# Token-sum rows split at every second first gate product, up weights tied from the 21st product on, two steps of the cached pieces moved to the sample block

## The chip, the cores and the metric

The kernel runs on one core of a Trainium2 chip. The metric is the device time of one execution in microseconds (us); lower is better. The engines are TensorE (PE, with its weight loads PEld), VectorE (DVE), ScalarE (ACT), GpSimd (POOL) and SyncE (SP), whose queue issues nearly all DMAs. Each engine works through its own instructions in order and waits for the others by semaphores.

## The reference

One inference step of a decoder layer, for 1024 prompt tokens and 64 sample tokens (8 sequences of 8), in float32. Cut to what matters:

```python
u = rms_norm(x, ln1)
a, q, k, v, g_a, g_b = split(u @ w_in)             # 512, 768, 768, 768, 1024, 1024 columns
q, k = rms_norm(heads(q), q_norm), rms_norm(heads(k), k_norm)     # 12 heads of 64
A = ((trailing_means(a) - a) @ lin per group) * pool_scale @ w_pa
# three groups of 4 heads: (window, dilation) = (128, 1), (512, 4), (2048, 16)
B = combine(dilated_window_attention(q, k, v)) @ w_pb  # sample tokens also read cached keys and values
h = x + (sigmoid(g_a) * A + sigmoid(g_b) * B) @ w_o
y = h + square(relu(rms_norm(h, ln2) @ w_up)) @ w_down           # 4096 hidden columns
```

It also returns the new pooling states and the updated key and value windows of both groups of tokens.

## The kernel before, in words

All 1088 tokens lie side by side as columns (features on the partitions). A float32 product is made of three passes over two halves of each operand: a high part, rounded by ACT (`split` L114, `put` L1255), and a low part, the difference, made by DVE (L115, L1256). The passes are high-high, high-low of one side, and high-low of the other; in the products of the later stages (`products`, L1248) the weights' low half is read in the last third of each half of the tokens.

The stages in order: the pooling input (PE at L319, to 61 us), q, k and v of the head groups 2, 1 and 0 with the attention woven in (61 to 383 us), the gates (383 to 580), A and B (L1566, to 653), the output projection (`ph`, to 751), the up projection (`pz`, to about 1096) and the down projection (`pd`, L2020, to the end). Gates, up and down use a two-by-two block scheme with seven block products, whose operands include sums and differences of the two token halves and of blocks of weights.

**What sets the order.** PE's instructions stand in the order of the code. The other engines' instructions are put in order by the framework's scheduler, from their dependencies and a timeline that it simulates. `behind_pe(ins)` adds a dependency: `ins` may not start before the matmul that was issued last in the code (`last_mm`). That is the kernel's means of keeping early work from crowding out urgent work.

**Group 0's blocks and the cached pieces.** The loop over blocks (L1137 and on) goes through (8, 0), 1, 2, 3, 4, 5, 6, 7: block 8 is the sample tokens, the others are 128 prompt tokens each. For each block the products of q, k and v are made (`qkv_part`), narrow ones one by one, wide ones (q and k together) for blocks 1 to 5. Behind each product DVE makes `ms`, POOL `mr` = ms ** -0.5 (L634), and ACT rescales with it (L639). `sample_own_keys` (L828 and on) is a generator that works through the sample tokens' cached keys of group 2 in 16 pieces, then their values in 16 pieces, one piece per step: it issues the two loads of the next piece, has POOL multiply the present one in four instructions (L839 `pck`, L863 `pcv`), and at the next step DVE adds it up (L841, L866, L867). Between keys and values lies a softmax (L849 to L854). `own_step` takes one step; the condition `own` says after which products (group, block, part 0/1/2 for q/k/v) it is taken.

**The gates.** `order` lists 16 first gate products, n = 0 to 15, which need no sums; at each, weights of product n + 3 are made ready (`raw_gf`), and the results are copied out (`g`, L1474). Meanwhile the four feature blocks k = 0 to 3 of the token sums are loaded (`fetch_sums`, tiles `gv` with one buffer each, k = 3 computed from x itself at L1325 to L1330) and split into the planes that the later gate products read (`split_sums`: four high and four low halves and a subtraction for each k). `split_t4` splits the eighth sum (`gt`). Then `gate_group` makes the other products, whose weights are sums (`sm_g`, L1400) put into `gapart` and `places` tiles. The attention's last part is woven into the first products; there PE's transpose `twg0u` (L760) reads `hl` (high half ACT L734, low half DVE L735).

**The up projection.** A queue of products is worked off by `run`, which prepares the weights three products ahead. Products 0 to 11 are the first two of each of six groups; 12 to 16 are the rest of group 0. `make_versions` at the start of the stage normalizes the second token half and makes its sums and differences in wide steps of 1088 columns (L1652, L1735, L115). The weights go through five places in turn (`up_spots`); their high halves (in `put_up`) and the weight sums (L1836, `sm`) are tied by `in_time`:

```python
    def in_time(ins):
        if begun[0] > 2:
            behind_pe(ins)
```

`begun[0]` is the number of the product being prepared, so before the change all but the first three wait for the product that PE was given last.

Of the kernel before, what the change touches and what calls it, by code (L numbers as in the profile page):

```python
# [36 lines left out]
def decoder_step(ctx, tc, i, o):  # L37
# [91 lines left out]
    def gate_quarter(f, a):  # L129
        return gate_panel(f).rearrange("p (k n) -> p k n", k=KD)[:, 4 * a:4 * a + 4, :P]  # L130
# [8 lines left out]
    def line_up(src, name, *after, width=None):  # L139


        wt = places[:, place[0] % 3]
        place[0] += 1
        width = width or src.shape[1]
        for a, key in zip(range(0, width, 512), after):
            coming_up.append(dict(width=width, src=src, name=name, a=a, key=key, wt=wt, raw=None))
        ask_ahead()
        return wt
# [33 lines left out]
    def behind_pe(ins, mm=None):  # L182

        tc.add_manual_dep(ins.ins, (mm or last_mm[0]).ins.name,
                          mybir.DependencyInfo(mybir.DependencyClass.Sync, mybir.DependencyReason.DATA), reason="pace")
# [361 lines left out]
    def step():  # L547
        for f in [later.pop(0) for _ in range(len(later))]:
            f()
        for r in list(active):  # L550
            if next(r, True):
                active.remove(r)
        cool[0] -= 1
        for r in waiting[:2]:
            if r not in primed:
                primed.add(r)
                next(r)
        if waiting and cool[0] <= 0:
            r = waiting.pop(0)
            if not next(r, True):  # L560
                active.append(r)
            cool[0] = 2

    def qkv_tiles(name, sample):
        qk = rr(ap1, [P, 512], F32, name=f"qk{name}", tag="qk", bufs=2)
        if sample:
            return qk, rr(ap1, [P, 256], F32, name=f"v{name}", tag="vs", bufs=2)
        return qk, rr(ap, [P, 256], F32, name=f"v{name}", tag="v", bufs=4)
# [16 lines left out]
    def in_order(blk):  # L585

        for s, copy in ((1, s_.copy), (0, v_.tensor_copy)):
            for k in range(0, KD, 2):
                t = natt[:, 4 * s + k // 2]
                copy(t.rearrange("p k (l r) -> p k l r", r=4),  # L590
                     act_t[s].rearrange("p k (r l) -> p k l r", r=4)[:, k:k + 2, blk * 32:(blk + 1) * 32, :].bitcast(F32))
                nat[s, k], nat[s, k + 1] = t[:, 0, :], t[:, 1, :]
# [484 lines left out]
    def own_step(every):  # L1077
        count[0] += 1
        if count[0] % every == 0:
            if next(own_keys, True) is not None and (2, "own") not in done:  # L1080
                done.add((2, "own"))
# [25 lines left out]
    for g in (2, 1, 0):  # L1107
# [39 lines left out]
        for blks in ((8, 0), (1,), (2,), (3,), (4,), (5,)) + (((6, 7),) if g else ((6,), (7,))):  # L1147

            if g and 6 in blks:
                next_wts = [(place[0] + j) % 3 for j in range(3)]  # L1150
                for j, after in enumerate((((7, 0), (6, 1), (6, 1), (7, 1)), ((7, 1), (6, 2), (6, 2), (7, 2)), ((7, 2),) * 4)):
                    line_up(i["w_in"][2 + 3 * j + g - 1], f"qkv{g - 1}_{j}", *((g,) + a for a in after))
            elif 7 in blks:
                wg_first = line_up(lambda a: gate_quarter(a // 512 % 2, a // 1024), "ga0",
                                   *((0, 7, j) for j in (0, 0, 1, 1)), width=2048)
            tiles = {b: qkv_tiles(f"{g}_{b}", b == 8) for b in blks}

            for js in (((0, 1), (2,)) if blks[0] in (1, 2, 3, 4, 5) else ((0,), (1,), (2,))):
                for b in (blks[::-1] if g == 0 and js == (2,) else blks):

                    own = g < 2 and b < 8 and (g, b, js) not in ((1, 7, (1,)), (1, 6, (2,)), (1, 7, (2,)))

                    def middle():
                        step()
                        if own:
                            own_step(1)

                    if g == 1 and extra and (1, "keys") in done:
                        extra = []
                        natt = np_.tile([P, 8, 2, P], F32R, name="natt", tag="nat")  # L1170
                        in_order(0)
                    wide = len(js) == 2
                    qkv_part(g, wts, b, f"{g}_{b}", tiles[b], js, middle if wide else None)
                    feed()
                    if own and not wide:
                        own_step(1)
                    if g < 2 and b == 8 and 0 in js:
                        dma(wrow, src_w)
                    if g == 0 and b == 8 and 2 in js:

                        sel = ap0.tile([P, 1024], F32R, name="sel", tag="smp")[:, :12 * HD]
                        behind_pe(v_.tensor_tensor(
                            sel.rearrange("p (a d) -> p a d", d=HD),
                            ident[:, :12].unsqueeze(2).to_broadcast([P, 12, HD]),
                            ident[:, 12:24].unsqueeze(2).to_broadcast([P, 12, HD]), op=ALU.add))
                    if 2 in js:
                        (sample_block if b == 8 else prompt_block)(g, b, *tiles[b])
                if g == 2 and 2 in js and 8 in blks:
                    start(pool_branch(), "p", now=True)
                    start(token_sums(), "t", now=True)  # L1190
# [76 lines left out]
    got, begun = {}, [0]  # L1267

    def in_time(ins):

        if begun[0] > 2:
            behind_pe(ins)

    def run(ahead=3):
# [33 lines left out]
    def fetch_sums(k):  # L1308
        if k == 3:
            rows_of[k] = [gx.tile([P, TOK], F32, name=f"gx{a}") for a in range(2)]  # L1310
            for a, x in enumerate(rows_of[k]):
                dma(x, i["xT"][:, 4 * a + k, :])
            return
        rows_of[k] = [rr(gx, [P, H], F32, name=f"gv{n}_{k}", tag=f"gv{n}", bufs=1) for n in range(3)]
        for t, slot in zip(rows_of[k], (0, 3, 1)):
            dma(t, ts_d[k][:, slot])

    def split_sums(k):

        v = rows_of[k]  # L1320
        if k == 3:
            v = [rr(gx, [P, H], F32, name=f"gv{n}_{k}", tag=f"gv{n}", bufs=1) for n in (0, 1, 3, 2)]
            for a, x in enumerate(rows_of[k]):
                for j in range(2):
                    v_.scalar_tensor_tensor(two(v[2 * a + j]), by_token(x, j), ln1[:, 4 * a + k:4 * a + k + 1], two(rb_g[j]),  # L1325
                                            op0=ALU.mult, op1=ALU.mult)
            v_.tensor_tensor(v[0], v[1], v[0], op=ALU.subtract)
            v_.tensor_tensor(v[1], v[3], v[1], op=ALU.subtract)
            v_.tensor_tensor(v[2], v[2], v[3], op=ALU.subtract)
            v_.tensor_tensor(v[2], v[2], v[0], op=ALU.add)  # L1330
            rows_of["t4", k] = v[2]
            v = [v[0], v[3], v[1]]
        for n, row in zip((1, "22", 3), v):
            behind_pe(split(*(t[:, k, :] for t in T[n]), row))
        v_.tensor_tensor(v[0], v[1], v[0], op=ALU.subtract)
        split(*(t[:, k, :] for t in T[2]), v[0])
# [129 lines left out]
    for n, (f, a) in enumerate(order):  # L1466
        fetch_first(n + 5)
        if a == 0:
            open_x[f] = bank_pair(f"pg{f}")
        products(open_x[f], ready.pop(n), B["21" if a else "11"], a == 0, between=step)  # L1470
        ready[n + 3] = put_first(n + 3)
        t = row_tile(1 + a, f)
        for c in range(2):
            s_.copy(two(t)[:, c], open_x[f][c][:, :Q])  # L1474
        dma_st(g_d[f, 0][:, half(0)] if a else pg_d[f], t)
        if n in (3, 6, 9, 11):
            split_sums({3: 0, 6: 1, 9: 3, 11: 2}[n])
        if n in (0, 2, 3, 6):
            fetch_sums({0: 0, 2: 3, 3: 1, 6: 2}[n])
        if n % 4 == 3 and psx is None and not active and not waiting:  # L1480
            finish_attention()
        if psx is not None and n > 7:
            prepare_main()
        if n == 13:
            for f in range(8):
                gate_group(f)
            for n_prep in range(3):
                got[n_prep] = queue[n_prep][0]()
        if n == 14:
            for load in loads.pop(0):  # L1490
                load()
# [669 lines left out]
```

## Time and profile before

| | before |
|---|---|
| time, median of 3 runs (lowest to highest) | 1442.21 us (1438.73 to 1447.19) |
| the profiled execution | 1438.98 us |
| its span, first to last instruction | 1437.2 us |
| DVE busy | 972.5 us (68%) |
| ACT busy | 759.1 us (53%) |
| POOL busy | 227.0 us (16%) |
| mean granted clock of TensorE | 0.994 |
| DMA | 300.01 MB, mean 209 GB/s |

Between the span and the time of that execution lie 1.8 us. The busy times are shares of the span; an engine that is busy for a small share can still be late at one place. The granted clock is the share of full speed that the chip's throttle allows TensorE.

### The profile page before, as it was taken

To read this page: it belongs to the slowest core of one execution; us is meant where nothing else is said; L and a number is where in the kernel's file an instruction comes from. 1 tells how busy PE (TensorE), PEld (TensorE's weight loads), DVE (VectorE), ACT (ScalarE), POOL (GpSimd) and SP (SyncE) were. 2 spreads that over 40 slices of the span, in tenths; PEclk is the share of its full clock that TensorE was granted. 3 is DMA by queue.
4 is the path that set the end of the run, shared out by engine and by line. 5 is a ranking of instruction groups with operands and counts; after the bars stand their busy time and mean duration, and the time that the engine had idled before them with its cause. 6 is when DMAs were issued, how large, how long until landed. Compare 5 with 4: busy or idle time off the path is not lost.

```text
span 1437.2 us, 29419 instructions
## 1 busy us (share of the span) xinstructions
PE 1413.6 (98%) x11101; PEld 1359.7 (95%) x11101; DVE 972.5 (68%) x1795; ACT 759.1 (53%) x1962; POOL 227.0 (16%) x291
## 2 busy tenths in 40 slices
PE   9999999999998999999999999999999999999998
PEld 8988977878898999999999999999999999999998
DVE  7688675666677676785558776656665686664556
ACT  8557755778655233573336455544554544444453
POOL 1711255556500000000001000000000000000100
PEclk9999999999999999999999999999999999999999
DMA  6322888744686676974548667567658987787684
GB/s 210 114 79 108 221 205 218 199 116 100 148 249 194 211 258 193 330 258 156 161 168 270 203 231 235 187 211 242 209 189 277 319 273 269 229 243 217 208 280 159
DMA packets 184203, 300.01 MB, mean 209 GB/s; under 512 B 34423, under 2 KB 91069, under 8 KB 182014
## 3 DMA queue, kind: packets, MB, share of 16 engines
q1 hardware_dynamic: 180990, 254.49, 57.4%
q0 software_dynamic: 3072, 43.65, 9.2%
q8 instruction: 87, 1.43, 0.4%
q14 instruction: 54, 0.44, 0.1%
HBM read 229.66 MB, written 112.06 MB: 238 GB/s over the span
## 4 chain that ended last, share of the span: by engine, by line
PE 84%; DMA 5%; DVE 5%; ACT 2%; issue 2%; POOL 1%; SPq 1%; DVEq 0%; ACTq 0%; POOLq 0%
PE pz L1248 22%; PE pd L2020 21%; PE pg L1248 10%; PE ph L194 7%; PE pqk L194 5%; PE pv L194 4%; PE a L319 3%; PE pab L1566 2%; PE pq L194 1%; PE pk L194 1%; DMA raw_qkv<-in_w_in_dram 1%; DVE act L115 1%; DVE places L1256 1%; PE pog0b L701 1%; PE sg0b L671 1%
## 5 line engine op out<-in xcount | busy, mean ns | idle before, releaser
L2020 PE MATMUL pd<-places 128*128 128x272 f32 x2688 | 335.0, 287 | 1.0 <-DVE places L1256 1.0
L2020 PEld LDWEIGHTS pd<-places 128*128 128x128 f32 x2688 | 334.7, 188 | 1.3 <-DVE places L1256 1.2
L1255 ACT ACTIVATE places<-raw_d 128x544 fp32r<-128x544 f32 (+1 forms) x176 | 111.0, 646 | 157.2 <-DMA raw_d<-z_d 48.0
L1256 DVE TENSOR_TENSOR places<-raw_d,places 128x544 fp32r<-128x544 f32 (+1 forms) x176 | 122.6, 711 | 89.9 <-ACT places L1255 88.3
L2059 POOL DMA_DIRECT2D out_kv_sample_dram<-in_cache_kv_dram x96 | 47.1, 491 | 836.5 <-ACT places L1255 518.0
L1248 PE MATMUL pz<-act,places 128*128 128x272 f32 x912 | 119.1, 289 | 0.0
L1248 PEld LDWEIGHTS pz<-act,places 128*128 128x128 f32 x912 | 116.5, 188 | 0.0
L194 PE MATMUL ph<-act,places 128*128 128x272 f32 x768 | 97.0, 288 | 0.0
L194 PEld LDWEIGHTS ph<-act,places 128*128 128x128 f32 x768 | 96.5, 188 | 0.1
L1248 PE MATMUL pz<-act,apart 128*128 128x272 f32 x624 | 84.1, 293 | 2.9 <-DVE apart L1256 2.8
L1248 PEld LDWEIGHTS pz<-act,apart 128*128 128x128 f32 x624 | 81.5, 192 | 3.5 <-DVE apart L1256 3.3
L1248 PE MATMUL pg<-act,places 128*128 128x272 f32 x576 | 78.0, 294 | 0.0
L1248 PEld LDWEIGHTS pg<-act,places 128*128 128x128 f32 x576 | 74.8, 191 | 0.7 <-issue 0.6
L634 POOL TENSOR_TENSOR mr<-ms,mhalf 128x4 f32<-128x4 f32 (+2 forms) x39 | 54.4, 1395 | 103.4 <-DVE ms L633 103.2
L194 PE MATMUL pqk<-places,act 128*128 128x512 f32 x240 | 61.0, 403 | 0.0
L1248 PE MATMUL pz<-places 128*128 128x272 f32 x432 | 56.4, 287 | 0.0
L1248 PEld LDWEIGHTS pz<-places 128*128 128x128 f32 x432 | 55.1, 188 | 0.0
L839 POOL TENSOR_TENSOR pck<-pck,qs 128x256 f32<-128x256 f32 x64 | 48.2, 786 | 42.4 <-DMA pck<-in_cache_kv_dram 26.8
L194 PEld LDWEIGHTS pqk<-places,act 128*128 128x128 f32 x240 | 44.6, 192 | 9.9 <-issue 0.2
L319 PE MATMUL a<-act,places 128*128 128x384 f32 (+1 forms) x288 | 50.3, 332 | 1.2 <-ACT act L297 1.2
L863 POOL TENSOR_TENSOR pcv<-pcv,sc 128x256 f32<-128x256 f32 x64 | 46.6, 760 | 27.9 <-DMA pcv<-in_cache_kv_dram 15.3
L1566 PE MATMUL pab<-ab,places 128*128 128x272 f32 x384 | 50.5, 287 | 0.0
(438 smaller groups left out, 2869.2 us busy)
## 6 DMA issues: line engine op xcount, KB each, us to landing
out_kv_sample_dram<-in_cache_kv_dram POOLq DMA_DIRECT2D x72, 480.0 KB, 5.0
raw_d<-z_d SPq DMA_DIRECT2D x112, 272.0 KB
z_d<-t SPq DMA_DIRECT2D x84, 272.0 KB
raw_d<-in_w_down_dram SPq DMA_DIRECT2D x80, 256.0 KB
raw_u<-in_w_up_dram SPq DMA_DIRECT2D x64, 256.0 KB
raw_qkv<-in_w_in_dram SPq DMA_DIRECT2D x36, 256.0 KB
pck<-in_cache_kv_dram SPq DMA_DIRECT2D x32, 256.0 KB
pcv<-in_cache_kv_dram SPq DMA_DIRECT2D x32, 256.0 KB
```

The lines of the kernel that those rows point to most:

```text
L115: v_.tensor_tensor(dst_lo, src, dst_hi.bitcast(F32), op=ALU.subtract)
L194: last_mm[0] = t_.matmul(out, lhs(a, k), rhs(b, k), start=(j == 0), stop=(j == len(terms) - 1))
L319: last_mm[0] = t_.matmul(pts[m][:, :n], wt[:, a, kk, m * P:(m + 1) * P], act4[b][kk][:, :, part4(c)], start=(p == 0 and kk == 0), stop=(p ...
L634: g_.tensor_tensor(r[:n, :H], ms[:n, :H], mhalf[:n, :H], op=ALU.pow)
L839: behind_pe(g_.tensor_tensor(t[:, n], t[:, n], qs[:, :256], op=ALU.mult))
L863: behind_pe(g_.tensor_tensor(tv, tv, sc[:, j + n, :].unsqueeze(2).to_broadcast([P, 4, HD]), op=ALU.mult))
L1248: last_mm[0] = t_.matmul(x[c][:, :Q], A[:, a, k * P:(k + 1) * P], Bv(b, k, c), start=(first and n == 0), stop=(n == len(terms) - 1), skip_ ...
L1255: ins = s_.activation(view(t[:, 0]), src, AF.Copy)
L1256: v_.tensor_tensor(view(t[:, 1]), src, view(t[:, 0]).bitcast(F32), op=ALU.subtract)
L1566: last_mm[0] = t_.matmul(q[x][:, c, :Q], w.rearrange("p s n -> p (s n)")[:, at:at + P], rhs, start=(n == 0), stop=(n == len(terms) - 1))
L2020: last_mm[0] = t_.matmul(chain[t][:, c, :Q], A[:, a, t * P:(t + 1) * P], Z[:, b, c * Q:(c + 1) * Q], start=(fresh and f == 0 and n == 0), ...
L2059: ins = g_.dma_start(d, a)
```

## The change

Three places are edited. First, `own` now holds after the sample block's q and k products of group 0, (0, 8, 0) and (0, 8, 1), and no longer after the k and v products of block 7, (0, 7, 1) and (0, 7, 2): every step in between is taken two products earlier, with its loads, POOL's products and DVE's additions. Second, `in_time` ties only what belongs to product 21 of the up stage and later (`begun[0]` counts from 0): the products numbered 3 to 20 are left to the scheduler, the data and the five places. Third, the token sums are split after the first gate products n = 3, 5, 7, 9 in the order k = 0, 1, 2, 3 (before: 3, 6, 9, 11 in the order 0, 1, 3, 2), and the rows of k = 2 are fetched at n = 5 instead of 6.

```diff
-                    own = g < 2 and b < 8 and (g, b, js) not in ((1, 7, (1,)), (1, 6, (2,)), (1, 7, (2,)))
+                    own = g < 2 and (g, b, js) in ((0, 8, (0,)), (0, 8, (1,))) or g < 2 and b < 8 and (g, b, js) not in (
+                        (1, 7, (1,)), (1, 6, (2,)), (1, 7, (2,)), (0, 7, (1,)), (0, 7, (2,)))
...
-        if begun[0] > 2:
+        if begun[0] > 20:
             behind_pe(ins)
...
-        if n in (3, 6, 9, 11):
-            split_sums({3: 0, 6: 1, 9: 3, 11: 2}[n])
-        if n in (0, 2, 3, 6):
-            fetch_sums({0: 0, 2: 3, 3: 1, 6: 2}[n])
+        if n in (3, 5, 7, 9):
+            split_sums((n - 3) // 2)
+        if n in (0, 2, 3, 5):
+            fetch_sums({0: 0, 2: 3, 3: 1, 5: 2}[n])
```

PE's instructions stand in the same order before and after; only those of the other engines move. Below, lines of the changed kernel from L1162 on are one higher than before.

POOL, at the sample block and block 0 of group 0 (`mr_8_0`, `mr_8_1`: the sample block's q and k; `mr_0_0`, `mr_0_1`: block 0's), before:

```order
L634 TENSOR_TENSOR mr_7_1_3523<-ms_7_1_3522,mhalf 128x4
L839 TENSOR_TENSOR pck_3490<-pck_3490,qs 128x256
L634 TENSOR_TENSOR mr_8_0_3703<-ms_8_0_3702,mhalf 64x4
L839 TENSOR_TENSOR pck_3490<-pck_3490,qs 128x256 x3
L634 TENSOR_TENSOR mr_0_0_3755<-ms_0_0_3754,mhalf 128x4
L634 TENSOR_TENSOR mr_8_1_3813<-ms_8_1_3812,mhalf 64x4
L634 TENSOR_TENSOR mr_0_1_3867<-ms_0_1_3866,mhalf 128x4
L863 TENSOR_TENSOR pcv_3786<-pcv_3786,sc 128x256 x4
L863 TENSOR_TENSOR pcv_3956<-pcv_3956,sc 128x256 x4
```

and POOL at the same place now:

```order
L634 TENSOR_TENSOR mr_7_1_3523<-ms_7_1_3522,mhalf 128x4
L839 TENSOR_TENSOR pck_3490<-pck_3490,qs 128x256 x4
L634 TENSOR_TENSOR mr_8_0_3703<-ms_8_0_3702,mhalf 64x4
L634 TENSOR_TENSOR mr_0_0_3763<-ms_0_0_3762,mhalf 128x4
L863 TENSOR_TENSOR pcv_3729<-pcv_3729,sc 128x256 x4
L634 TENSOR_TENSOR mr_8_1_3823<-ms_8_1_3822,mhalf 64x4
L863 TENSOR_TENSOR pcv_3851<-pcv_3851,sc 128x256 x4
L634 TENSOR_TENSOR mr_0_1_3884<-ms_0_1_3883,mhalf 128x4
L863 TENSOR_TENSOR pcv_3897<-pcv_3897,sc 128x256 x4
L863 TENSOR_TENSOR pcv_3973<-pcv_3973,sc 128x256 x4
```

The first two groups of four value products (`pcv`) now stand ahead of the two `mr` of k, with the last key piece whole ahead of `mr_8_0`. At block 7 the two groups that stood between its `mr` of q and its `mr` of k are gone.

DVE, at the end of the first gate products (`gv_3`: the sums of k = 3; `gapart`: weights of the first product that reads the sums), before:

```order
L1256 TENSOR_TENSOR gapart_5871<-sm_g_0_6080,gapart_5871 128x512
L1256 TENSOR_TENSOR places<-sm_g_0_6088,places 128x512
L1256 TENSOR_TENSOR places<-rawg_1_5876,places 128x512
L1327 TENSOR_TENSOR gv_3_5914<-gv_3_5915,gv_3_5914 128x544
L1256 TENSOR_TENSOR gapart_5872<-sm_g_0_6084,gapart_5872 128x512
L1328 TENSOR_TENSOR gv_3_5915<-gv_3_5917,gv_3_5915 128x544
L1330 TENSOR_TENSOR gv_3_5916<-gv_3_5916,gv_3_5914 128x544
L115 TENSOR_TENSOR act_78<-gv_3_5914,act_77 128x544
L115 TENSOR_TENSOR places<-gv_3_5915,places 128x544
L1335 TENSOR_TENSOR gv_3_5914<-gv_3_5917,gv_3_5914 128x544
L115 TENSOR_TENSOR gt_1_5874<-gv_3_5916,gt_0_5873 128x544
L115 TENSOR_TENSOR places<-gv_3_5914,places 128x544
```

and DVE at the same place now:

```order
L115 TENSOR_TENSOR places<-gv_3_5924,places 128x544
L1257 TENSOR_TENSOR places<-raw_gf_1_5890,places 128x512
L1336 TENSOR_TENSOR gv_3_5923<-gv_3_5926,gv_3_5923 128x544
L115 TENSOR_TENSOR gt_1_5883<-t_1_5946,gt_0_5882 128x544
L1257 TENSOR_TENSOR places<-raw_gf_1_5948,places 128x512
L115 TENSOR_TENSOR gt_1_5883<-t_2_6012,gt_0_5882 128x544
L115 TENSOR_TENSOR places<-gv_3_5923,places 128x544
L1401 TENSOR_TENSOR sm_g_0_6080<-rawg_0_5884,rawg_1_5885 128x512
L1401 TENSOR_TENSOR sm_g_0_6088<-rawg_0_5884 128x512
L1401 TENSOR_TENSOR sm_g_0_6084<-sm_g_0_6080,rawg_0_5884 128x512
L115 TENSOR_TENSOR gt_1_5883<-gv_3_5925,gt_0_5882 128x544
L1257 TENSOR_TENSOR gapart_5880<-sm_g_0_6080,gapart_5880 128x512
```

The last products of the sums stood behind the low half in `gapart`; now all of them stand ahead of it.

ACT and DVE also take a split of k = 1 (`gv_1` to `places`) ahead of the two halves of `hl` now, and DVE the two other splits of k = 1 and their subtraction ahead of the attention's next product.

DVE, in the up stage behind `make_versions` (`sm_0`: weight sums of group 0; `apart`: product 12's weights; steps of 1088 columns are the wide ones), before:

```order
L115 TENSOR_TENSOR places<-u_9496,places 128x1088
L1735 TENSOR_TENSOR y_0_8331<-y_0_8331,u_9496 128x1088
L1836 TENSOR_TENSOR sm_0_9793<-raw_u_0_9661,raw_u_1_9662 128x512
L115 TENSOR_TENSOR places<-u_9496,places 128x1088
L1735 TENSOR_TENSOR y_0_8331<-y_0_8331,u_9496 128x1088
L1836 TENSOR_TENSOR sm_0_9825<-sm_0_9793,raw_u_0_9661 128x512
L115 TENSOR_TENSOR t_1_9492<-y_0_8331,t_0_9491 128x1088
L1836 TENSOR_TENSOR sm_0_9861<-raw_u_0_9661 128x512
L1256 TENSOR_TENSOR apart_9406<-sm_0_9793,apart_9406 128x512
```

and DVE at the same place now:

```order
L115 TENSOR_TENSOR places<-u_9496,places 128x1088
L1736 TENSOR_TENSOR y_0_8331<-y_0_8331,u_9496 128x1088
L1837 TENSOR_TENSOR sm_0_9825<-sm_0_9793,raw_u_0_9661 128x512
L1257 TENSOR_TENSOR places<-sm_0_9861,places 128x512
L1257 TENSOR_TENSOR apart_9406<-sm_0_9793,apart_9406 128x512
L115 TENSOR_TENSOR places<-u_9496,places 128x1088
L1736 TENSOR_TENSOR y_0_8331<-y_0_8331,u_9496 128x1088
L115 TENSOR_TENSOR t_1_9492<-y_0_8331,t_0_9491 128x1088
L1257 TENSOR_TENSOR apart_9407<-sm_0_9825,apart_9407 128x512
```

Ahead of product 12's low half there now stand three wide steps fewer: the second part of `places<-u`, the second of `y_0<-y_0,u` and the first of `t_1`. Further up, two of the weights' low halves (`raw_uf`) have moved from behind the normalization (L1652) to ahead of it.

## The prediction

> **What bounds the kernel now.** The page was read first, then PE's own waits, then PE's timeline around each long wait and the clock that it was granted there, and last the queues of the engines that it waited for. On the page:
>
> ```profile
> PE 1413.6 (98%) x11101; PEld 1359.7 (95%) x11101; DVE 972.5 (68%) x1795; ACT 759.1 (53%) x1962; POOL 227.0 (16%) x291
> ```
>
> TensorE has work for 98% of the span, so only what holds PE up can move the end. These are its longest waits (us in total, times, longest):
>
> ```profile
> PE pg L1248 <- ACT act L114: 4.1, 1, 4.1
> PE pz L1248 <- DVE apart L1256: 2.8, 1, 2.8
> PE sg0b L671 <- ACT pTg0b L693: 2.6, 1, 2.6
> PE twg0u L760 <- DVE hl L735: 1.7, 1, 1.7
> ```
>
> Three of them are near the three edits. PE's timeline (start, duration, engine, line, matmuls merged; in brackets the idle time before, and what ended it) shows what stands around them:
>
> ```profile
> 386.33 0.48 PE L671 MATMUL sg0b<-qkTg0b,qkTg0b 64*128 64x128 f32 x2 [0.63 <-DVE qkTg0b L657]
> 389.45 0.58 PE L671 MATMUL sg0b<-qkTg0b,qkTg0b 64*128 64x128 f32 x1 [2.63 <-ACT pTg0b L693]
> ...
> 391.45 3.09 PE L1248 MATMUL pg<-act,places 128*128 128x272 f32 x12
> ...
> 396.72 1.76 PE L1248 MATMUL pg<-act,places 128*128 128x272 f32 x12
> ...
> 452.21 0.53 PE L1248 MATMUL pg<-act,gapart 128*128 128x272 f32 x3
> 456.86 1.27 PE L1248 MATMUL pg<-act,gapart 128*128 128x272 f32 x4 [4.11 <-ACT act L114]
> ...
> 466.05 3.17 PE L1248 MATMUL pg<-places 128*128 128x272 f32 x24
> 469.06 3.19 PE L1248 MATMUL pg<-act,places 128*128 128x272 f32 x24
> ...
> 790.53 1.26 PE L1248 MATMUL pz<-act,apart 128*128 128x272 f32 x8
> 794.63 3.75 PE L1248 MATMUL pz<-act,apart 128*128 128x272 f32 x16 [2.84 <-DVE apart L1256]
> 798.23 3.18 PE L1248 MATMUL pz<-places,apart 128*128 128x272 f32 x24
> ```
>
> Twelve gate matmuls take 1.76 us at 396.72 and 3.09 at 391.45, just after a wait. The columns of the next answer are the stretch, its length, the busy time of PE, PEld, DVE, ACT and POOL, the granted clock, and the DMA:
>
> ```profile
> 389.00:396.00 7.00, 6.55 (x44) 6.14 (x46) 4.11 (x14) 3.63 (x12) 0.00 (x0) 0.56 0.48 134
> 457.00:464.00 7.00, 6.46 (x29) 6.14 (x30) 5.32 (x9) 2.56 (x4) 0.00 (x0) 0.54 0.02 9
> 795.00:798.50 3.50, 3.50 (x19) 3.50 (x19) 2.06 (x4) 0.07 (x1) 0.00 (x0) 0.58 0.85 295
> ```
>
> The clock is 0.56, 0.54 and 0.58 right behind three of these waits, against 0.994 over the run. Each wait costs itself and a slow stretch behind it.
>
> **The Trainium skill on that clock.** The Trainium skill ("TensorE: Matmul & The Clock Gate", section "HAM oscillation — how this bites in real kernels") asks only that PE has no idle gaps above about 3.4 us. Here waits of 2.63 and 2.84 us were followed by a slow stretch too, so the trace decides, and the sum below takes the slow stretch as gone wherever its wait goes; by the skill only the one behind the 4.11 us wait would go. It speaks against counting on the rest, and has a rival below.
>
> **Part 1: two value pieces leave block 7 for the sample block.** The wait of 2.63 us is put down to ACT's copy of pTg0b. ACT, POOL and DVE at that place:
>
> ```profile
> 381.67 0.23 DVE L633 TENSOR_SCALAR ms<-ms,xeps 128x4 f32<-128x4 f32 x1 [0.51 <-ACT qk L630]
> 383.44 3.55 POOL L863 TENSOR_TENSOR pcv<-pcv,sc 128x256 f32<-128x256 f32 x4 [0.99 <-PE tpg0b L690]
> 386.95 1.00 POOL L634 TENSOR_TENSOR mr<-ms,mhalf 128x4 f32<-128x4 f32 x1
> 387.99 0.93 ACT L639 ACTIVATE qk<-pk,mr 128x64 f32<-128x64 f32 x4 [2.10 <-POOL mr L634]
> ```
>
> POOL multiplies a group of four value pieces (L863) from 383.44 to 386.99 and only then computes mr (L634), although its input ms was ready at 381.9. ACT waits 2.10 us for mr, and its copies of pTg0b stand behind. In the changed order nothing stands between the mr of q and that of k in block 7, so mr can be done by 383, and ACT's copies follow PE's transposes at once. Lost now: the two waits 0.63 + 2.63, the twelve matmuls 3.09 − 1.76 = 1.33, and the scores from 389.45 to 391.45 at about half pace, some 1.0 (an estimate by the granted 0.56): 5.6 us. What is late next is DVE's copy of qkTg0b, the 0.63 us wait. I take 5.0 back; the bounds are 0 (something else holds ACT there) and 5.6.
>
> The pieces are paid for in the sample block. There two groups of four now stand ahead of the mr of k, one before the sample's and one before block 0's:
>
> ```profile
> 286.81 1.00 POOL L634 TENSOR_TENSOR mr<-ms,mhalf 64x4 f32<-64x4 f32 x1 [1.18 <-DVE ms L633]
> 289.41 0.94 ACT L639 ACTIVATE qk<-pk,mr 64x64 f32<-64x64 f32 x4
> 313.04 2.33 POOL L863 TENSOR_TENSOR pcv<-pcv,sc 128x256 f32<-128x256 f32 x4 [3.99 <-DMA pcv<-in_cache_kv_dram]
> ```
>
> A group takes 2.33 us (313.04) to 3.55 (383.44), and POOL was idle for 1.18 us ahead of the sample's mr (286.81), so that mr ends 1.2 to 2.4 us later than at 287.8; block 0's follows likewise. ACT's rescaling (L639) takes it up at 289.41, so 1.6 us of lateness is covered by work that stands ahead in ACT's queue. Behind a late mr are queued on ACT the other rescalings and the copies of pTg1b, and PE waits for those: for the PSUM bank that a rescaling frees, and for pTg1b in its values product. I take 1.5 us lost, nearer to the covered end than to a whole group of 3.55; the bounds are 0.5 gained (POOL is less crowded later) and 7 lost (a first group held by a landing as late as the 3.99 at 313.04 and its own 2.33, less the 1.6, and the second's 2.33).
>
> Each step also issues the two loads of a later piece. On SP's queue two of them now stand ahead of the last quarter of group 0's v weights, which PE wants a product later; I count that within the 1.5 and the 7. At block 7 two loads fewer stand among those of the first gate weights (raw_ga), which can only help. The other pieces move one block earlier, with the same neighbours in each block: nothing.
>
> **Part 2: the token sums are split at every second product.** From 452.21 to 466.05 PE does two products, 24 matmuls each, in 13.84 us. One takes 469.06 − 466.05 = 3.01 from start to start, so 13.84 − 6.02 = 7.8 us are lost. PE waits for the splits of the last sum, which DVE does last:
>
> ```profile
> 411.00:464.00 53.00, 46.66 (x355) 45.68 (x354) 40.22 (x67) 28.90 (x64) 0.00 (x0) 0.94 0.68 207
> 426.00:441.00 15.00, 15.00 (x122) 15.00 (x121) 9.17 (x15) 7.69 (x19) 0.00 (x0) 1.00 0.84 253
> 457.92 0.71 DVE L115 TENSOR_TENSOR act<-gv,act 128x544 fp32r<-128x544 f32 x1
> ```
>
> DVE is idle for 15.0 − 9.17 = 5.8 us between 426 and 441, yet the split that PE waits for comes at 457.92. In the changed order the sums' work fills that hole: k = 1 is split one product earlier, k = 2 four earlier (as the third, before k = 3), and DVE's rows for k = 3 all stand before the weights' low half (gapart) of the first product that reads the sums. Does it fit? From 411 to 464 DVE is busy for 40.2 us, a few of them for later products. PE wants that low half a third into the product, at 452.21 + 1.0, so 42.2 us are there. It fits, narrowly; the loads of k = 2's rows now wait on SP for the tiles of k = 1, and the gate weights' loads queue behind them, which are asked for five products ahead. I leave 0.5 us of waiting and take 7.3 back; bounds 3 (DVE held for 3 us, with a short slow stretch) and 7.8.
>
> It has a price at 421, where PE's transpose twg0u waits 1.7 us (above) for hl, whose two halves are
>
> ```profile
> 420.35 0.21 ACT L734 CAST hl<-cw 128x24 fp32r<-128x24 f32 x1
> 420.82 0.18 DVE L735 TENSOR_TENSOR hl<-cw,hl 128x24 fp32r<-128x24 f32 x1
> ```
>
> Now a split of k = 1 (0.66 us on ACT and 0.72 on DVE) stands before each half. ACT reaches it at 420.5, DVE can follow at 421.1, and hl comes at about 421.75 instead of 420.82: 0.9 us more for PE, a wait of 2.6. The load that this split reads is the first of its three, and I take it as landed. I take 0.9 lost; bounds 0 and 4.0 (with a slow stretch, 7 us at 0.56, so 3.1).
>
> **Part 3: up weights are free of PE until the 21st product.** From 790.53 to 798.23 PE does 24 matmuls in 7.70 us where 3.01 would do: 4.7 lost. DVE is the cause:
>
> ```profile
> 760.00:790.00 30.00, 29.98 (x238) 29.74 (x237) 29.09 (x32) 21.32 (x32) 2.02 (x4) 1.00 0.92 292
> 792.09 1.28 DVE L115 TENSOR_TENSOR t<-y,t 128x1088 fp32r<-128x1088 f32 x1
> 793.30 0.68 DVE L1836 TENSOR_TENSOR sm<-raw_u 128x512 f32<-128x512 f32 x1
> 793.90 0.68 DVE L1256 TENSOR_TENSOR apart<-sm,apart 128x512 fp32r<-128x512 f32 x1
> ```
>
> It is busy for 29.09 of 30 us, and the low half that PE waits for starts at 793.90. Untied, the weights' steps move up among the wide ones. Counted in the two orders from the normalization on, 17 wide steps and 12 narrow ones stood up to and with that low half; now 14 and 10 do. A wide step takes 793.30 − 792.09 = 1.2 us, a narrow one 0.6: 3 × 1.2 + 2 × 0.6 = 4.8 us earlier, a start at 789.1. PE needs it at 790.53 + 1.0: no wait. The next product's low half follows three wide steps later, done at 794.0, needed at 794.5. I take 4.5 back; bounds 3 and 4.7. The steps that moved ahead of the normalization fall in ACT's and DVE's idle time there.
>
> **The sum.** 5.0 − 1.5 + 7.3 − 0.9 + 4.5 = 14.4 us. The profiled execution took 1438.98 us (span 1437.2); less 14.4 is 1424.6. It was among the fastest shown: the median of three is 1442.21, 3.2 us above. Part of that is presumably the waits themselves, so I add 1.4, not 3.2: 1426.0 us.
>
> **Rivals.** (A) The longer wait at 421 is followed by a slow stretch: 3.1 us more, 1429. For it: 2.63 us did it once; against: the 1.7 us of before did not. (B) The slow stretches at 389 and 795 are not made by the short waits. Then 5.6 − 3.26 = 2.3 and 4.7 − 2.84 = 1.9 us stay: 1430. This is what the skill's rule would make of it; against it stand two stretches out of two. (C) A long wait stays although its cause was moved: with part 2 undone by DVE's full queue 1433; with parts 1 and 2 both, 1438, which is no change. (D) Slower: the value pieces hold the sample block. POOL works in order, so each mr behind a group waits for that group's landing and its products: 3.99 + 3.55 = 7.5 us, twice, each followed by a slow stretch of 3.1: 21.3 us. The pieces would then be as late as before at block 7, so part 1 gives nothing, and the time is 1426.0 + 5.0 − 1.5 + 21.3 = 1451. For it: POOL has waited for landings; against: the pieces there are loaded a step ahead. Once these holds cost PE over 11 us (7.3 + 4.5 − 0.9), the kernel is no faster.
>
> **The numbers.** About 0.5% (7.2 us) is what a measurement of this kernel can tell from no change, so "faster" is below 1435.0 and "slower" above 1449.4. Forecast 0.52 (1421 to 1430), A 0.12, B 0.05, C with one wait 0.09, C with two 0.09, D mild (about 1440) 0.04, D in full 0.09. Faster: 0.52 + 0.12 + 0.05 + 0.09 = 0.78; same 0.09 + 0.04 = 0.13; slower 0.09. The range is 1420 to 1438: the low end lets every term reach its better bound, 1424.6 − 0.6 − 0.5 − 0.2 − 0.9 − 2.0 = 1420.4; the high end takes in A, B and C and leaves out D.
>
> **What would show it.** Right: PE's waits no longer list pg for act, pz for apart or sg0b for pTg0b above 1 us; the clock is 1.00 in the stretches that answer to 389 to 396, 457 to 464 and 795 to 798.5; twg0u waits for hl about 2.6 us; up to 383 the two traces differ by under 3 us. Wrong: a clock below 0.9 in the sample block, new waits of PE for act or gapart near 452, or a stage without edits (580 to 750, or beyond 800) that takes another time.

## The result, and the profile after

The changed kernel takes 1433.08 us (median of 6, 1430.98 to 1435.61) beside 1442.93 for the kernel before on the same chip: ratio 0.9933, 95% interval 0.9910 to 0.9956. A second set gave 1432.36 beside 1440.16, ratio 0.9941 (0.9923 to 0.9958). The ratio's difference from 1, times 1440 us, is 9.6 and 8.5 us gained, where the sum of the terms said 14.4. The profiled execution took 1434.28 us (span 1432.1), only 4.7 less than that of before, so what the two traces show place by place adds up to about 5 us.

PE's line of the page after:

```profile
PE 1410.9 (99%) x11101; PEld 1358.0 (95%) x11101; DVE 976.4 (68%) x1795; ACT 758.7 (53%) x1962; POOL 225.5 (16%) x291
```

and PE's longest waits (us in total, times, longest), after:

```profile
PE pv L194 <- ACT qk L639: 2.8, 1, 2.8
PE twg0u L760 <- DVE hl L735: 2.5, 1, 2.5
PE sg0b L671 <- DVE qkTg0b L657: 2.5, 1, 2.5
PE pg L1249 <- ACT g L1475: 2.4, 1, 2.4
```

None of the four is one of the three waits that the edits aimed at; those are gone. PE's timeline at the three places, after:

```profile
388.50 0.49 PE L671 MATMUL sg0b<-qkTg0b,qkTg0b 64*128 64x128 f32 x2
389.40 0.37 PE L671 MATMUL sg0b<-qkTg0b,qkTg0b 64*128 64x128 f32 x1 [0.42 <-ACT pTg0b L693]
390.48 1.77 PE L1249 MATMUL pg<-act,places 128*128 128x272 f32 x12
...
458.79 3.15 PE L1249 MATMUL pg<-act,gapart 128*128 128x272 f32 x24
461.78 3.16 PE L1249 MATMUL pg<-places,gapart 128*128 128x272 f32 x24
...
788.91 3.15 PE L1249 MATMUL pz<-act,apart 128*128 128x272 f32 x24
793.48 2.28 PE L1249 MATMUL pz<-places,apart 128*128 128x272 f32 x16 [0.42 <-DVE apart L1257]
```

The scores wait 0.42 us for pTg0b instead of 2.63, and the twelve matmuls behind them take 1.77 instead of 3.09. The first products that read the sums follow each other without a gap, 2.99 us apart. The first up product whose weights are sums no longer waits for `apart` (2.84 before); the next one waits 0.42. But PE's timeline now has four stops elsewhere:

```profile
286.65 5.49 PE L194 MATMUL pv<-places,natt 128*128 128x256 f32 x24 [2.82 <-ACT qk L639]
...
400.96 0.49 PE L671 MATMUL sg0b<-qkTg0b,qkTg0b 64*128 64x128 f32 x4 [2.52 <-DVE qkTg0b L657]
402.06 3.09 PE L1249 MATMUL pg<-act,places 128*128 128x272 f32 x12
...
423.46 0.38 PE L760 MATMUL twg0u<-cst,hl 128*24 128x128 f32 x2 [2.54 <-DVE hl L735]
...
439.05 5.18 PE L1249 MATMUL pg<-act,places 128*128 128x272 f32 x27 [2.42 <-ACT g L1475]
```

and this is the granted clock (the last but two of the columns) behind each of them, and at two of the old places:

```profile
286.00:292.80 6.80, 6.15 (x28) 5.83 (x30) 6.72 (x19) 6.80 (x37) 6.10 (x9) 0.50 0.70 136
402.00:405.40 3.40, 3.40 (x18) 2.95 (x14) 2.90 (x16) 2.26 (x9) 0.00 (x0) 0.51 0.95 243
423.50:427.00 3.50, 3.50 (x29) 3.48 (x30) 1.07 (x2) 0.66 (x1) 0.00 (x0) 1.00 1.00 346
439.60:443.00 3.40, 3.40 (x17) 3.40 (x16) 3.40 (x6) 2.29 (x5) 0.00 (x0) 0.50 0.87 297
389.00:394.00 5.00, 4.60 (x49) 4.18 (x50) 3.86 (x13) 3.67 (x13) 0.00 (x0) 1.00 0.81 235
455.00:465.00 10.00, 10.00 (x82) 10.00 (x81) 6.11 (x11) 4.56 (x10) 0.00 (x0) 1.00 0.74 235
```

The clock is 0.50 behind three of the four, 1.00 behind the wait of 2.54 us, and 1.00 at these two places where it had been slow before. So three stalls went, and three of the same kind, a little shorter, came.

PE does the same matmuls in the same order in both kernels, so each one's start can be compared. By the times of before, PE lost 3.2 us from 283 to 300, won 5.6 from 380 to 397, lost 4.1 from 400 to 410, 0.9 at `twg0u` and 4.2 from 430 to 440, and won 7.9 from 452 to 466 and 4.0 from 790 to 850. Together that is 5.1 us won, the difference of the two spans.

**Where the new stalls come from.** At 286.65 PE wants the bank that ACT's rescaling frees. ACT's timeline, after and then before:

```profile
284.37 0.63 ACT L114 ACTIVATE places<-raw_qkv 128x512 fp32r<-128x512 f32 x1 [3.46 <-DMA raw_qkv<-in_w_in_dram]
285.69 0.90 ACT L639 ACTIVATE qk<-pq,mr 64x64 f32<-64x64 f32 x4
```

```profile
280.62 0.63 ACT L114 ACTIVATE places<-raw_qkv 128x512 fp32r<-128x512 f32 x1 [0.40 <-DMA raw_qkv<-in_w_in_dram]
```

The rescaling stands behind a split of the last quarter of the v weights, which came 3.75 us later. SP's queue, after and then before, shows why:

```profile
276.93 1.30 SPq L825 DMA_DIRECT2D pcv<-in_cache_kv_dram  x2
278.33 0.55 SPq L123 DMA_DIRECT2D raw_qkv<-in_w_in_dram  x1
```

```profile
277.31 0.34 SPq L123 DMA_DIRECT2D raw_qkv<-in_w_in_dram  x1
281.31 1.27 SPq L825 DMA_DIRECT2D pcv<-in_cache_kv_dram  x2
```

The two loads of a value piece (64x4x256 floats each, 0.52 MB together) now stand ahead of that quarter. It is issued 1.0 us later and lands 3.75 us later, presumably since 0.52 MB that had followed it now go first. (An estimate: at the 238 GB/s that the DMA moved from that issue to the split, 0.52 MB take 2.2 us.) POOL, whose hold the prediction had priced here, cost PE nothing:

```profile
287.54 2.50 POOL L863 TENSOR_TENSOR pcv<-pcv,sc 128x256 f32<-128x256 f32 x4
290.21 1.42 POOL L634 TENSOR_TENSOR mr<-ms,mhalf 64x4 f32<-64x4 f32 x1 [0.17 <-DVE ms L633]
```

It did the group of four and then still waited 0.17 us for its input. Its next group did hold block 0's `mr`: the input was there at 293.38, `mr` began at 294.12, and ACT waited 0.35 us for it. But PE's timeline shows no wait from there to 313 us.

At 400.96 the scores wait for DVE's copy of qkTg0b. DVE after, and then before:

```profile
399.40 1.17 DVE L1326 SCALAR_TENSOR_TENSOR gv<-gx,cols,rb_g 128x544 f32<-128x544 f32 x1 [4.26 <-DMA gx<-in_xT_dram]
400.49 0.42 DVE L657 COPY qkTg0b<-tqg0b 128x256 f32<-128x256 f32 x1
```

```profile
397.66 0.42 DVE L657 COPY qkTg0b<-tqg0b 128x256 f32<-128x256 f32 x1
...
401.24 1.21 DVE L1325 SCALAR_TENSOR_TENSOR gv<-gx,cols,rb_g 128x544 f32<-128x544 f32 x1 [0.63 <-DMA gx<-in_xT_dram]
```

In the changed kernel DVE stood 4.26 us before an instruction of the token sums whose input `gx` had not landed, with the copy behind it. Before, that instruction stood seven places behind the copy on DVE; now it stands right ahead of it. With part 1 alone it stands right ahead as well, with part 2 or part 3 alone behind it as before, so it is part 1 that moved the row past the copy.

At 439.05 it is ACT's copy of `g` that is late:

```profile
424.56 5.83 SPq L1317 DMA_DIRECT2D gv<-ts_d  x2
```

in SP's queue, and in ACT's timeline

```profile
437.26 0.66 ACT L114 ACTIVATE act<-gv 128x544 fp32r<-128x544 f32 x1 [3.04 <-DMA gv<-ts_d]
```

SP's loads of the rows for k = 2 wait for the one buffer of k = 1 (5.83 us for two issues), ACT then 3.04 us for the rows, and its copies of `g` stand behind. Of SP's 5.83 us, 4.8 are a wait for DVE's subtraction in `gv` (L1336).

### The profile page after: what moved, and what is told of

It is laid out like the page before. It is cut to its first block, busy times and chain, and to the rows that moved or that the text cites. A ratio compares the mean times of both kernels' runs of the same rounds, so it can differ in the third digit from the quotient of the medians.

```text
span 1432.1 us, 29419 instructions
## 1 busy us (share of the span) xinstructions
PE 1410.9 (99%) x11101; PEld 1358.0 (95%) x11101; DVE 976.4 (68%) x1795; ACT 758.7 (53%) x1962; POOL 225.5 (16%) x291
## 4 chain that ended last, share of the span: by engine, by line
PE 85%; DMA 6%; DVE 4%; ACT 2%; issue 2%; SPq 1%; POOL 1%; DVEq 0%; ACTq 0%; POOLq 0%
PE pz L1249 22%; PE pd L2021 21%; PE pg L1249 10%; PE ph L194 7%; PE pqk L194 6%; PE pv L194 4%; PE a L319 3%; PE pab L1567 2%; PE pq L194 1%; PE pk L194 1%; DMA gg<-g_d 1%; DMA gv<-ts_d 1%; DVE places L115 1%; DVE act L115 1%; DMA out_yT_dram<-row 1%
## 5 line engine op out<-in xcount | busy, mean ns | idle before, releaser
L319 PEld LDWEIGHTS a<-act,places 128*128 128x128 f32 x288 | 47.5, 188 | 3.0 <-ACT act L297 1.9
```

What stands on the lines that cost most here:

```text
L319: last_mm[0] = t_.matmul(pts[m][:, :n], wt[:, a, kk, m * P:(m + 1) * P], act4[b][kk][:, :, part4(c)], start=(p == 0 and kk == 0), stop=(p ...
```

## The experiments

All were timed in five rounds against the kernel before, whose medians in the sets were 1439.1 to 1440.2 us. The last column is the ratio's difference from 1, times 1440 us. The intervals in brackets are 3 to 6 us wide, so most neighbours in the table overlap.

| kernel | ratio (95%) | us against before |
|---|---|---|
| part 1 alone | 1.0007 (0.9993 to 1.0020) | +1.0 |
| part 2 alone | 0.9967 (0.9955 to 0.9978) | -4.8 |
| part 3 alone | 0.9962 (0.9948 to 0.9976) | -5.5 |
| parts 2 and 3 | 0.9927 (0.9914 to 0.9940) | -10.5 |
| the changed kernel again | 0.9941 (0.9923 to 0.9958) | -8.5 |
| changed, value pieces a product later | 0.9926 (0.9911 to 0.9942) | -10.7 |
| changed, row of the sums tied | 0.9918 (0.9899 to 0.9937) | -11.8 |
| changed, both repairs | 0.9905 (0.9888 to 0.9923) | -13.7 |
| part 1 alone, both repairs | 0.9989 (0.9976 to 1.0001) | -1.6 |
| both repairs, splits at 3, 6, 8, 9 | 0.9911 (0.9897 to 0.9924) | -12.8 |
| the same, second buffer | 0.9889 (0.9876 to 0.9902) | -16.0 |
| both repairs, second buffer, splits as changed | 0.9914 (0.9901 to 0.9928) | -12.4 |

**Each part alone.** The edits are those of the diff above, one at a time.

> The kernel before with part 1 alone (two value pieces leave block 7 for the sample block). Theory 1, the recorded terms: 5.0 - 1.5 = 3.5 us faster. Theory 2, read off the trace of after: the wait and slow stretch at 386 to 395 go (3.4 to 5 us), but the two loads ahead of the last quarter of v weights cost PE a wait of about 2.8 us and a slow stretch of 2.4 near 285, and the first scaled row of the token sums, now nine places earlier in DVE's queue and ahead of the copy of qkTg0b, costs a wait of about 2.5 us near 400: together 0 to 3 us slower or no change. The profile should show both new waits although parts 2 and 3 are absent.

> The kernel before with part 2 alone (token sums split at every second product). Theory 1, the recorded terms: 7.3 - 0.9 = 6.4 us faster. Theory 2, read off the trace of after: the loss at 452 to 466 goes (6.6 us), twg0u waits 2.5 instead of 1.7 us, and a new wait of gate products for ACT near 440 costs 2.4 us and a slow stretch of 1.5: 2 to 3 us faster. In its profile the first row of the sums stands behind the copy of qkTg0b, so sg0b has no wait of 2.5 us near 400.

> The kernel before with part 3 alone (up weights tied to PE from the 21st product on). Both theories: 4.1 to 4.7 us faster, the wait of pz for apart near 790 below 1 us, all else as before. A rival, that the slow stretch there is not made by the wait: 1.9 us less of it, 2.8 us faster.

Part 1 gave nothing, against 3.5 us by its terms. Its waits of PE, without parts 2 and 3:

```profile
PE sg0b L671 <- DVE qkTg0b L657: 3.6, 1, 3.6
PE pv L194 <- ACT qk L639: 3.3, 1, 3.3
```

and DVE's timeline near 400, where the copy follows at 404.28:

```profile
403.19 1.17 DVE L1326 SCALAR_TENSOR_TENSOR gv<-gx,cols,rb_g 128x544 f32<-128x544 f32 x1 [5.37 <-DMA gx<-in_xT_dram]
```

Both new stalls are its own. Part 2 gave 4.8 (3.2 to 6.5) against 6.4 by the terms and 2 to 3 by the second theory, and its profile has no wait of PE for ACT's `g` of 0.5 us or more, so the one at 439 in the changed kernel is not a fixed price. Part 3 gave 5.5 (3.5 to 7.5) against 4.5. With part 3 alone the wait of pz for `apart` was 0.7 us. The rival's 2.8 us is below its interval.

**Without part 1, and the changed kernel again.** Only the condition `own` is put back as it was before, parts 2 and 3 stay.

> The changed kernel without part 1: parts 2 and 3 as they are, the value pieces as in the kernel before. If the parts add up as measured alone (4.7 and 5.0 us): 9 to 10 us faster than the kernel before, the same as the changed kernel, with the wait of sg0b for pTg0b back (2.1 to 2.6 us) and none near 285 or of 2.5 us near 400. If part 1 pays as the recorded terms say: 3.5 us slower than the changed kernel.

> The changed kernel once more, unedited, as the measure for the runs beside it on the same chip. If the three parts add up as they were measured one by one (0.0, 4.7 and 5.0 us), it is 9 to 10 us faster than the kernel before; by the recorded terms it would be 14.

The parts add up: 10.5 us without part 1, 8.5 to 9.6 with it, intervals overlapping. Part 1 as written is worth nothing, or a little less than nothing. Without it, PE's wait of the scores for pTg0b is back (2.1 us), and there is none near 285 or 400.

**The value pieces one product later.** This undoes SP's order at the v weights and keeps block 7 free.

```diff
-                    own = g < 2 and (g, b, js) in ((0, 8, (0,)), (0, 8, (1,))) or g < 2 and b < 8 and (g, b, js) not in (
+                    own = g < 2 and (g, b, js) in ((0, 8, (1,)), (0, 8, (2,))) or g < 2 and b < 8 and (g, b, js) not in (
```

> The changed kernel, with the two value pieces placed one product later each in the sample block (behind its second and third product instead of its first and second), so that SP has the last quarter of group 0's v weights ahead of the pieces' loads, as before. If SP's order makes the wait near 285: PE's wait of 2.8 us for ACT's rescaling goes and so does the slow clock behind it, 3 to 5 us faster than the changed kernel (about 15 us faster than the kernel before by medians). If POOL's group of multiplications ahead of the mr of k makes it: the wait stays or moves to block 0, no gain over the changed kernel.

SP's queue in this kernel:

```profile
277.23 0.34 SPq L123 DMA_DIRECT2D raw_qkv<-in_w_in_dram  x1
280.71 1.27 SPq L825 DMA_DIRECT2D pcv<-in_cache_kv_dram  x2
```

ACT's split of the quarter:

```profile
280.21 0.63 ACT L114 ACTIVATE places<-raw_qkv 128x512 fp32r<-128x512 f32 x1 [0.59 <-DMA raw_qkv<-in_w_in_dram]
```

PE's values product:

```profile
283.58 3.04 PE L194 MATMUL pv<-places,natt 128*128 128x256 f32 x24
```

The quarter is issued first again, and `pv` follows without a wait, 24 matmuls in 3.04 us instead of 5.49. So SP's order made that stall; POOL's groups move with the edit too, but they had cost PE no wait. The time, 10.7 us less than before, is nearer to the changed kernel's 8.5 to 9.6 than the 15 that was expected, and cannot be told from it. Two things stand against the gain in the profile: the other stall, the scores' wait for the copy of qkTg0b, was 3.6 us this time, and the edit brings a wait of its own, 1.1 us for ACT's rescaling at 292, which all six kernels with it show.

**The row of the sums tied to PE.** One instruction gets a dependency on the matmul issued last in the code, so that it stands behind the copy:

```diff
+                    if (a, j) == (1, 0):
+                        behind_pe(ins)
```

> The changed kernel, with one scaled row of the token sums' last part (gv3, the one that had slipped ahead of the copy of qkTg0b in DVE's queue) tied to the matmul last written before it, so that it stands behind that copy and much later. If DVE's wait for the row's input makes the wait of sg0b near 400: that wait (2.5 to 3.6 us) falls below 1 us and 2.5 to 5 us are gained on the changed kernel, the more the more often a slow stretch follows it. The rival, that the scores are held by the copy of qkTg0b for another reason (its transposes, or ACT's half of it): the wait stays above 2 us.

> The changed kernel with both repairs: the value pieces one product later in the sample block, and the scaled row tied to PE. If the two new waits (near 285 and near 400) are all that part 1 lost: 5 to 9 us faster than the changed kernel, 15 to 18 us faster than the kernel before, and PE's waits list none above 2 us but twg0u for hl.

With the tie alone: 1427.53 us beside 1432.36 of the changed kernel in the same set, 4.8 less; the wait of the scores for the copy is no longer among PE's waits of 0.4 us or more, and that for the v weights is still there (2.8 us). With both repairs 1425.97, 6.4 less than the changed kernel, and PE's longest waits are

```profile
PE twg0u L760 <- DVE hl L735: 2.5, 1, 2.5
PE pg L1249 <- ACT g L1477: 1.4, 2, 0.8
```

In that profile the granted clock is 1.000 over the whole span. It is 13.7 us faster than before, a little short of the 15 expected. The two stalls are most of what part 1 had lost: with them repaired the kernel is ahead of the 10.5 us without part 1, though the intervals overlap.

**Part 1 with its repairs, alone.**

> The kernel before with part 1 alone, and both repairs. If part 1 was a right idea that paid for itself with two avoidable waits: 3.5 to 5 us faster than the kernel before, where part 1 as written gave nothing. If freeing block 7 is worth nothing in itself: no change.

It gave 1.6 us (0.1 slower to 3.5 faster): less than 3.5 to 5, though its profile has no wait of PE over 0.7 us from 300 to 410. Its later stall was larger, for a second reason that DVE's timeline shows:

```profile
788.93 1.29 DVE L1738 TENSOR_TENSOR y<-y,u 128x1088 f32<-128x1088 f32 x1 [1.36 <-DMA y<-u_d]
```

and in the kernel with part 1 alone:

```profile
793.65 1.29 DVE L1736 TENSOR_TENSOR y<-y,u 128x1088 f32<-128x1088 f32 x1 [2.07 <-DMA y<-u_d]
```

PE waited 4.0 us there instead of 2.8. DVE waited 1.36 and 2.07 us for a load from `u_d`; in the kernel before it waited for no load there. With part 3 in place PE's wait there is at most 0.9 us. Why that load lands late was not tried, and stays open. So repaired, part 1 is worth some 3 us beside parts 2 and 3 (13.7 against 10.5, though the intervals overlap), and it is not shown that it pays alone.

**What remains: the wait of `twg0u`.**

```diff
-        if n in (3, 5, 7, 9):
-            split_sums((n - 3) // 2)
-        if n in (0, 2, 3, 5):
-            fetch_sums({0: 0, 2: 3, 3: 1, 5: 2}[n])
+        if n in (3, 6, 8, 9):
+            split_sums({3: 0, 6: 1, 8: 2, 9: 3}[n])
+        if n in (0, 2, 3, 6):
+            fetch_sums({0: 0, 2: 3, 3: 1, 6: 2}[n])
```

> The changed kernel with both repairs, and the token sums split at products 3, 6, 8 and 9 instead of 3, 5, 7 and 9 (the second fetched again at 6), so that no split of the second sum stands ahead of hl. If those splits make twg0u's longer wait: it falls from 2.5 to 1.7 us, no slow stretch follows it, and 1 to 2.5 us are gained on the kernel with both repairs, 15 to 17 us on the kernel before. The price, if DVE no longer gets done before the first product that reads the sums: a new wait near 450 of 1 us or more, and nothing gained.

The wait of `twg0u` is 1.7 us again, so the splits made the rest of it; but the time did not fall (12.8 against 13.7 us, intervals overlapping), and PE still waited for ACT's copies of `g` (1.3 us in two waits) and 0.7 us for `gapart`. Then `gv` of the first row with `bufs=2` instead of 1, with these splits and with those of the change:

> The same, with two buffers instead of one for the first of a sum's three rows, so that SP does not stand waiting for that tile with the other rows' loads and the gate weights' behind it (two waiting loads held SP from 424.56 to 430.39 in the changed kernel). If those late rows hold ACT and its evictions: PE's waits of pg for ACT's evictions near 430 to 445 (0.8 to 2.4 us) go, 1 to 2 us faster than without. If they land in time by chance most of the time: no difference.

> The changed kernel with both repairs and two buffers for the first of a sum's three rows, but with the splits at products 3, 5, 7 and 9 as changed. If the second buffer alone makes the last gain: as fast as with the splits at 3, 6, 8 and 9 beside it (15.3 us faster than the kernel before by medians), with the wait of twg0u at 2.5 us again. If the two need each other: 14 us, as with the repairs alone.

With both, 1424.40 us beside 1439.72 (ratio 0.9889, 0.9876 to 0.9902): the fastest version of all, clock 1.000, and the longest waits of PE are

```profile
PE twg0u L760 <- DVE hl L735: 1.7, 1, 1.7
PE a L319 <- ACT act L297: 1.3, 2, 0.9
```

PE no longer waits for copies of `g` by more than 0.4 us. It is 3.2 us faster than without the buffer, more than the 1 to 2 expected, the intervals just overlapping. The second buffer alone gained nothing (12.4): there `twg0u` waited 3.2 us. By the medians both together gave what neither gave alone; beside the two repairs alone (13.7) the gain is not shown, for those intervals overlap widely.

## Why the prediction was right or wrong

- **Parts 2 and 3: right in mechanism and about in size.** 4.8 and 5.5 us measured, 6.4 and 4.5 forecast, both forecasts within the measured intervals; the two together 10.5 against 10.9. Both DVE readings (work moved into an idle stretch; weights moved up among the wide steps) came out at the places named: in the two traces PE won 7.9 us from 452 to 466, where 7.3 were forecast, and 4.0 from 790 on, where 4.5 were. One term of part 2 was sized too low. The rows of k = 2 that wait on SP for the tiles of k = 1 were seen and given 0.5 us; in the profiled execution they made the wait of 2.42 us at 439 and a slow stretch, 4.2 us together. In the second profile of the changed kernel, and with part 2 alone, they made no such wait.
- **The price at 421: right, and rival A was rated too low.** `twg0u` waited 2.54 us, 2.6 were said. A slow stretch followed it in five of the eight profiles with a wait of 2.5 us or more, where A had a chance of 0.12; behind the 1.7 us of before and of five experiments none did.
- **Part 1's gain: right where it was looked for.** All of the waits at 386 to 395 but 0.42 us went, and the slow stretch with them. From the scores at 386.33 to the matmuls at 396.72 PE had taken 10.39 us; now it takes 5.59 (388.50 to 394.09). That is 4.8 us won, where 5.0 were forecast.
- **Part 1's price: the failed step.** "I take 1.5 us lost" was a sum over POOL's groups. The loads on SP were seen ("two of them now stand ahead of the last quarter of group 0's v weights, which PE wants a product later") and counted within it without a price. A product later is 3 us; the quarter came 3.75 us later. The stall cost 2.82 us of wait and 5.49 - 3.04 = 2.45 of slow matmuls; some of that came back just behind it, where PE before had waited 1.1 us for pTg1b, so that 3.2 us were lost by 300, more than twice the 1.5.
- **A second price was not looked for.** The order of DVE was read where the edits are, not where the scheduler would answer them. The row of the sums that slipped ahead of the copy cost 2.52 us of wait and 3.09 - 1.76 = 1.33 of slow matmuls. With these two, part 1's 3.5 us became nothing, which is most of the 4.8 to 5.9 us between 14.4 and what was measured. In the profile they outweigh its gain: 3.2 and 4.1 us lost, 5.6 won.
- **The rivals.** D, the slower case, had the right place and the wrong engine: the sample block did pay, through SP's queue and not through POOL. B, that slow stretches are not made by short waits, fell: at all three places the slow stretch went with the wait, and three of the four new waits brought one.
- **The signs.** At block 7 the traces differ by 2.2 us (scores at 386.33, now at 388.50), under the 3 us that were said; but right behind the stall the difference had been 4.3 us (PE's transposes tpg1b at 287.64, now at 291.93). The stages without edits took the same time, as said: from 466 to 751 and from 850 to 1400 the difference stays within 0.1 us. A clock below 0.9 in the sample block, named as a sign of being wrong, was there, and it led to the failed step. The time, 1433.08, lies 7.1 us above the forecast and inside the range.
- **The 1.4 us added for the median** was about right: later sets of the kernel before had medians of 1439.1 to 1440.2, close to the profiled 1438.98; the three runs' 1442.21 was high.

## What to carry to other kernels

When a step is moved, price each queue that it joins by what stands directly behind it there. Here a load behind two others was issued 1.0 us later and landed 3.75 us later, so the issue time alone is too low a price. Where a scheduler fills the queues, compare the whole order of the two programs for instructions far from the edit that moved past one that the bound engine waits for, and tie those whose inputs come by DMA. A removed stall only counts if the next ones do not grow: in the fastest version here PE never waits more than 1.7 us at a time, and its clock stayed at 1.00.

## What the runs showed of the hardware

The slow clock comes in stretches of 3.41 or 6.83 us, whose starts lie on one grid of 3.41 us within each execution, and by these profiles what they go by is how long PE idles within one step of that grid, not how long the wait is. The two kernels that follow have the same wait of 2.54 us. With part 2 alone, PE's timeline:

```profile
420.31 0.58 PE L760 MATMUL twg0u<-cst,hl 128*24 128x128 f32 x2 [2.54 <-DVE hl L735]
```

and two steps of the grid (stretch, length, busy time of PE first, the granted clock ahead of the DMA's two):

```profile
416.27:419.68 3.41, 1.50 (x12) 1.28 (x11) 2.47 (x8) 2.00 (x7) 0.00 (x0) 1.00 1.03 249
419.68:423.09 3.41, 2.78 (x13) 2.74 (x14) 1.62 (x4) 0.66 (x1) 0.00 (x0) 0.50 1.02 347
```

With both repairs, PE's timeline and then three steps:

```profile
417.47 0.38 PE L760 MATMUL twg0u<-cst,hl 128*24 128x128 f32 x2 [2.54 <-DVE hl L735]
```

```profile
412.28:415.69 3.41, 2.64 (x21) 2.42 (x20) 2.58 (x9) 2.24 (x7) 0.00 (x0) 1.00 1.03 214
415.69:419.11 3.42, 1.64 (x14) 1.66 (x15) 1.90 (x4) 1.54 (x4) 0.00 (x0) 1.00 1.10 306
419.11:422.52 3.41, 3.41 (x29) 3.41 (x29) 1.66 (x3) 1.66 (x4) 0.00 (x0) 1.00 0.88 312
```

In the first PE was busy for 1.50 of 3.41 us in one step, idle for 1.91, and the next step ran at 0.50. In the second the wait fell across an edge: idle for 0.77 and 1.78, and the clock stayed at 1.00. The changed kernel's own two profiles differ in the same way: `twg0u` waited 2.54 us in one, with the clock at 1.00 behind it, and 2.55 us in the other, with 1.95 us of idle in one step and a slow step next. In the fourteen profiles, behind the first 10 us of each, a slow step followed every one of the 25 full-clock steps with 1.9 us of idle or more, and one of the nine with 1.6 to 1.8. (In the first 10 us two steps with 1.5 and 1.7 were followed by one.) A stretch was two steps long where PE idled 0.65 us or more in its first step, and one step long at 0.63 or less. So a wait of about 2 to 2.6 us takes a slow stretch with it or not by chance, from one execution to the next; by the rows further up that is worth 1.3 to 2.5 us. The Trainium skill ("TensorE: Matmul & The Clock Gate") describes, in its Part 1 on the HAM clock gate, an activity window of 3413 ns that runs on freely; the grid agrees with that. The rule in its section "HAM oscillation — how this bites in real kernels", of gaps above about 3.4 us, does not hold here: waits of 2.42 and 2.52 us were enough.
